# Tying a decoder block's background steps behind the newest weight piece

## The chip, the cores and the metric

The kernel runs on one core of one Trainium2 chip. The metric is the device time of one execution in microseconds. A core has engines that run side by side, each in its own program order: PE (TensorE) multiplies matrices and transposes, DVE (VectorE) and ACT (ScalarE) work on elements, POOL (GpSimd) does a few small things, SP issues most of the DMAs. They wait for each other by semaphores, so an instruction that is not ready holds up everything behind it on its engine.

## The reference

One decoder block for 256 tokens of width 2048, all in float32:

```python
mod = silu(c) @ w_ada + b_ada                  # 6 vectors of 2048
h = rmsnorm(x, g0) * (1 + sc_m) + sh_m
q, k, v, g_ret, u, gate_r, gate_s = split(h @ w_in)   # 1024 1024 2048 2048 1024 2048 2048
ret = head_group_norm(retention(rope(q), rope(k) * 128**-0.5, v))     # 8 heads
y_ret = (silu(g_ret) * ret) @ w_ret_out
y_ssm = gelu(s5_ssm(u, ...))                   # 64 groups of 16 channels, 64 complex states each
a, b = split(y_ssm @ w_s5_glu)
y = (sigmoid(gate_r) * y_ret + sigmoid(gate_s) * a * sigmoid(b)) @ w_out
x = x + gt_m * rmsnorm(y, g1)
h = rmsnorm(x, g2) * (1 + sc_f) + sh_f
a, b = split(h @ w_ffn_in)                     # 5632 each
x = x + gt_f * rmsnorm((silu(a) * b) @ w_ffn_out, g3)
```

## The kernel before

**Weight pieces.** Nearly all of the time goes into dense products with weights that are read once. A weight matrix is cut into pieces of 256 rows by 512 columns (512 KB). For one piece, `split_piece` issues the DMA into `raw` from SP, ACT copies it into a rounded part `hi` (L290), DVE subtracts to get the rest `lo` (the helper at L80), and `products` issues 12 matmuls: for each of the 2 blocks of 128 rows and 2 blocks of 128 tokens one on `hi` (L302), one of the activations' rest on `hi` (L303) and one on `lo` (L306). There are 3 buffers each of `hi` and `lo`, 5 of `raw`, 4 PSUM banks for products (`mm`) and 4 for everything else (transposes and small products).

**Stages.** The inner dimension of w_in is taken in three groups (`KG`), since the normalized input `h` becomes ready in three parts. In each group the columns in `EARLY` are multiplied; partial sums lie in the `spill` tiles, and the third group adds the last part to them in `early_evac`. There u is transposed (`uT`) and laid out for the S5 branch (`u_blocks`, 32 copies into `uS` on POOL, L852), q and k go through the rotary step (`rope_t`: on DVE two products into `rb`, one product and one sum on `spill`, for each of two token blocks, then four transposes into `ps_qk` on PE and a copy by ACT), and g_ret is gated and transposed (`ps_r`). The third group runs in the trace from about 235 to 400 us; then comes what is called the S5 stage here (gate r, w_ret_out and gate s, to about 720 us), then w_s5_glu and w_out, the second norm, and the FFN.

**Background.** Work that is not a weight piece is written as generators in two lanes. `mix` holds the S5 set-up (`s5_prep`), `u_blocks`, the retention heads (`heads`: scores `ps_s`, mask `sT`, outputs `ps_o`, statistics `bst` and `bag`) and the S5 groups (`s5_group`, eight of them, with small products `ps_bt`, `ps_v`, `ps_k`, `ps_y`). `ada` holds the modulation vectors: rows of w_ada come by DMA into `araw`, and DVE adds them up into `acc` (L202). After each piece `piece_done` ticks both lanes: each has a rate, and for each whole credit one step is issued. Deferred evacuations of finished columns (`later`) are issued three pieces after their column's end.

**The order.** A scheduler places each engine's instructions; the order in which the code issues them is its priority, and an instruction can move ahead of ones issued before it when it is thought to be ready earlier. `tc.issue_after(ins)` ties what is issued inside it behind `ins`. Before the change nothing in `piece_done` is tied.

Of the kernel before, what the change touches and what calls it, by code (L numbers as in the profile page):

```python
# [14 lines left out]
AF = mybir.ActivationFunctionType  # L15
# [37 lines left out]
def hybrid_block(ctx: ExitStack, tc: tile.TileContext, A, out, dbg=None):  # L53
# [25 lines left out]
    def tt(o, a, b, op):  # L79
        V.tensor_tensor(o, a, b, op=op)  # L80

    def slot(shape, dt, name):
        return slots.tile(shape, dt, tag="slot", name=name)
# [36 lines left out]
            while gen in self.gens:  # L120
                self.step()

    mix, ada = Lane(), Lane()

    def tick():
        mix.tick()
        ada.tick()

    late = []

# [154 lines left out]
    def split_piece(w, k0, KP, c0, keep=None, kept=None, tag="hi", hi=None):  # L285
        raw = wp.tile([P, KP, CW], F32, tag="raw", name="raw", bufs=RB)
        nc.sync.dma_start(raw, w[k0 * P:(k0 + KP) * P, c0:c0 + CW].rearrange("(k p) n -> p k n", p=P))
        if hi is None:
            hi = wp.tile([P, KP, CW], F32R, tag=tag, name="hi")
        S.activation(hi, raw, AF.Copy)  # L290
        lo = kept
        if lo is None:
            lo = keep if keep is not None else wp.tile([P, KP, CW], F32R, tag="lo", name="lo")
            tt(lo, raw, hi.bitcast(F32), ALU.subtract)
        return hi, lo

    def products(pst, lhs, hi, lo, k0, KP, ka, kb, toks):
        for k in range(KP):
            kt = k0 + k
            for t in toks:  # L300
                xh, xl = lhs(kt, t)
                T.matmul(pst[t], xh, hi[:, k, :], start=kt == ka, stop=False)  # L302
                T.matmul(pst[t], xl, hi[:, k, :], start=False, stop=False)  # L303
            for t in toks:
                xh, xl = lhs(kt, t)
                T.matmul(pst[t], xh, lo[:, k, :], start=False, stop=kt == kb - 1)  # L306

    later = []

# [2 lines left out]
            later.pop(0)[1]()  # L312

    def piece_done():
        tick()
        for it in later:
            it[0] -= 1
        while later and later[0][0] <= 0:
            later.pop(0)[1]()

    def defer(fn, *args):
        later.append([DEFER, lambda: fn(*args)])

    def mm_tile():
        return pmm.tile([P, CW], F32, tag="mm", name="mm")
# [330 lines left out]
    def s5_group(e):  # L656
# [12 lines left out]
        for g in range(2):  # L669
            pp = slice(64 * g, 64 * g + 64)  # L670
            S.activation(B4[pp, :, :, :, g, :].rearrange("p r t d h -> p (r t) d h"),
                         bp[pp].rearrange("p d r t h -> p (r t) d h"), AF.Copy)
            S.activation(B0[pp, :, :, g, :], bs[pp, e], AF.Copy)
            S.activation(CB[pp, :, :, 1:4, g, :].rearrange("p r t d h -> p (r t) d h"),
                         cp[pp].rearrange("p d r t h -> p (r t) d h"), AF.Copy)
            S.activation(CB[pp, :, :, 0, g, :], Cc[pp, e], AF.Copy)

        def mat(x, ri, t):
            return x[:, ri, t].rearrange("p d g h -> p (d g h)")
# [88 lines left out]
            yield  # L768

    def s5_all():  # L770
        yS.append(slot([P, 4, 4, 4, 32], F32, "yS"))
        for e in range(8):
            if e % 4 == 0:
                yield from s5_table(e // 4)
            yield from s5_group(e)
        dump("y", yS[0])
        yield from s5_out()
# [10 lines left out]
    def rope_t(src, dst):  # L788
        rope = ret[1]
        for t in range(2):  # L790
            sv = src[:, t, :].rearrange("p (h w d) -> p h w d", h=4, w=2)
            rb = ev("rb").rearrange("p (h w d) -> p h w d", h=4, w=2)
            for w in range(2):
                tt(rb[:, :, w, :], sv[:, :, 1 - w, :],
                   rope[:, t, 1:2, w * 64:w * 64 + 64].to_broadcast([P, 4, 64]), ALU.mult)
            s3 = src[:, t, :].rearrange("p (h d) -> p h d", h=4)
            tt(s3, s3, rope[:, t, 0:1, :].to_broadcast([P, 4, P]), ALU.mult)
            tt(src[:, t, :], src[:, t, :], rb.rearrange("p h w d -> p (h w d)"), ALU.add)
            ps = trp("ps_qk")
            for i in range(4):  # L800
                T.transpose(ps[:, i * P:(i + 1) * P], src[:, t, i * P:(i + 1) * P], ident)
            S.activation(dst[:, :, t * P:(t + 1) * P], ps.rearrange("p (i q) -> p i q", i=4), AF.Copy)

    def heads(hf, qk, vs):
        for i in range(4):
# [38 lines left out]
    def u_blocks(uT):  # L844
        uS.append(slot([P, NS, 64], F32, "uS"))
        uv = uS[0].rearrange("p (q ih v i) s -> p ih i v q s", q=4, ih=2, v=2)
        for i in range(4):
            for r in range(4):
                for v in range(2):
                    src = uT[32 * i:32 * i + 32, v].rearrange("p q (s r) -> p r q s", r=4)[:, r]  # L850
                    dst = uv[32 * (3 - r):32 * (3 - r) + 32, i // 2, i % 2, v]
                    G.tensor_copy(dst, src)  # L852
                yield

    def early_evac(gi, ci, pst):
# [12 lines left out]
        if ci == 1:  # L868
            uT = slot([P, 2, 4, NT], F32, "uT")
            for n in range(2):  # L870
                for t in range(2):
                    ps = trp("ps_u")
                    for i in range(4):
                        T.transpose(ps[:, i * P:(i + 1) * P], spill[0][:, n, t, i * P:(i + 1) * P], ident)
                    S.activation(uT[:, n, :, t * P:(t + 1) * P], ps.rearrange("p (i q) -> p i q", i=4), AF.Copy)
            mix.add(u_blocks(uT))
        if ci in (2, 3, 6, 7):
            if ci in (2, 6):
                keep["qk"] = slot([P, 2, 4, NT], F32, "qk")
            rope_t(sp, keep["qk"][:, ci % 2])  # L880
        if ci in (5, 9):
            hf = ci // 8
            vs[hf] = [spill[ci // 2][:, k] for k in range(2)]
# [36 lines left out]
    for gi, (k0, k1) in enumerate(KG):  # L920
        if gi + 1 < len(KG):
            nxt = ada_group(*KG[gi + 1])
            ada.add(nxt)
            ada.rate = 34 / (AR[gi] * NG[gi] * ((k1 - k0 + 1) // 2))
            if gi == 0:
                mix.add(prep)
                mix.rate = 0.14
        else:
            first_ctx.close()
            ret_tiles()  # L930
            af = ada.add(ada_f())
            ada.rate = 0.35
            mix.rate = 0.75
        for ci, off in enumerate(EARLY):
            if ci >= NG[gi]:
                continue
            g0 = gi
            while g0 and ci >= NG[g0 - 1]:
                g0 -= 1
            pst = linear(w_in, off, KG[g0][0], k1, h)  # L940
            defer(early_evac, gi, ci, pst)
        if gi + 1 < len(KG):
            ada.finish(nxt)
            flush()
            make_h(*KG[gi + 1])
            if gi == len(KG) - 2:
                mix.finish(prep)
# [4 lines left out]
    s5 = s5_all()  # L952
    s5_tiles()
    mix.add(s5)
    ada.rate = 0.5
    mix.rate = 0.75
    Mt = [slot([P, D], F32, "M") for _ in range(2)]

    def gate_evac(dst, n, pst):
# [232 lines left out]
```

## Time and profile before

| what | value |
|---|---|
| time, median of 3 runs | 1646.94 us (1644.99 to 1647.46) |
| profiled execution | 1647.59 us |
| its span in the trace | 1645.8 us |
| PE busy | 1592.4 us, 97% |
| PEld (weight loads of PE) | 1300.4 us, 79% |
| DVE busy | 1182.9 us, 72% |
| ACT busy | 780.8 us, 47% |
| POOL busy | 63.4 us, 4% |

The span is the time from the first to the last instruction that the profiler saw; 1.8 us of the profiled execution lie outside it. PE is busy nearly always, so what can be gained without taking work off PE is the 53.4 us of its span in which it is not busy, and what its clock loses.

### The profile page before, as it was taken

Reading aid. Unit: us, or ns where it says so; the run is one execution under the profiler, and the core shown is the slowest. Engines: PE = TensorE matmul, PEld = TensorE weight load, DVE = VectorE, ACT = ScalarE, POOL = GpSimd, SP = SyncE. Lnnn points to the kernel's source line nnn. Section 1 sums busy time; section 2 is a strip of 40 time slices with the busy share of each in tenths; the row PEclk is TensorE's granted clock in tenths of the full one; section 3 lists DMA queues with packets and bytes.
Section 4 is the critical chain, followed back from the end, with each engine's and each line's share of the span. In section 5 each row is a group of like instructions: output and inputs, shape, how many; then the busy total and the mean of one; then the engine's idle time right before and its main releaser. Section 6 shows DMA issues by size and latency. Waiting matters only on the chain.

```text
span 1645.8 us, 20564 instructions
## 1 busy us (share of the span) xinstructions
PE 1592.4 (97%) x7475; PEld 1300.4 (79%) x7475; DVE 1182.9 (72%) x1585; ACT 780.8 (47%) x1070; POOL 63.4 (4%) x84
## 2 busy tenths in 40 slices
PE   5999998999999999999998999999999999999997
PEld 2788886888778778788886788888888888888886
DVE  7889989888878988789966676477554455444454
ACT  4464443454656466544446544444444444344342
POOL 0200008010000000000000000000000000000000
PEclk9999999999999999999999999999999999999999
DMA  9999875765776867899985788688666666666663
GB/s 352 349 366 337 312 234 179 257 193 175 250 228 206 263 198 238 270 319 328 331 298 183 241 273 306 191 278 271 191 206 193 190 191 191 188 193 192 194 194 128
DMA packets 184005, 398.12 MB, mean 242 GB/s; under 512 B 12760, under 2 KB 14144, under 8 KB 183392
## 3 DMA queue, kind: packets, MB, share of 16 engines
q1 hardware_dynamic: 183360, 395.67, 73.7%
q0 software_dynamic: 544, 1.15, 0.3%
q8 instruction: 58, 0.95, 0.2%
q14 instruction: 43, 0.35, 0.1%
HBM read 394.67 MB, written 2.10 MB: 241 GB/s over the span
## 4 chain that ended last, share of the span: by engine, by line
PE 78%; DVE 8%; DMA 7%; issue 3%; ACT 2%; POOL 0%; SPq 0%; DVEq 0%; POOLq 0%; ACTq 0%
PE mm L306 25%; PE mm L302 25%; PE mm L303 25%; DMA araw<-in_w_ada_dram 4%; DVE lo L80 3%; DMA fraw<-in_w_ada_dram 1%; ACT hi L290 1%; DMA raw<-in_w_in_dram 1%; DVE acc L202 1%; DVE spill L80 1%; PE ps_a L1124 1%; PE ps_v L692 1%; DVE q L80 1%; DMA xs<-in_x_dram 0%; ACT Tz L701 0%
## 5 line engine op out<-in xcount | busy, mean ns | idle before, releaser
L290 ACT ACTIVATE hi<-raw 128x1024 fp32r<-128x1024 f32 x539 | 569.5, 1061 | 687.0 <-PE mm L303 611.9
L80 DVE TENSOR_TENSOR lo<-raw,hi 128x1024 fp32r<-128x1024 f32 x519 | 634.4, 1227 | 339.6 <-ACT hi L290 339.0
L302 PE MATMUL mm<-hi,h 128*128 128x512 f32 x1408 | 556.1, 395 | 1.9 <-ACT hi L290 1.3
L303 PE MATMUL mm<-hi,h 128*128 128x512 f32 x1408 | 550.4, 391 | 2.0 <-DVE h L80 2.0
L306 PE MATMUL mm<-lo,h 128*128 128x512 f32 x1376 | 426.9, 391 | 3.3 <-DVE lo L80 3.2
L302 PEld LDWEIGHTS mm<-hi,h 128*128 128x128 f32 x1408 | 265.2, 188 | 58.0 <-ACT hi L290 2.1
L303 PEld LDWEIGHTS mm<-hi,h 128*128 128x128 f32 x1408 | 265.4, 189 | 55.8 <-DVE h L80 2.4
L306 PEld LDWEIGHTS mm<-lo,h 128*128 128x128 f32 x1376 | 258.3, 188 | 61.7 <-DVE lo L80 7.4
L202 DVE SCALAR_TENSOR_TENSOR acc<-araw,cT,acc 128x1024 f32<-128x1024 f32 (+1 forms) x150 | 177.0, 1180 | 36.4 <-DMA araw<-in_w_ada_dram 36.2
L303 PE MATMUL mm<-hi,aT 128*128 128x512 f32 x348 | 135.5, 389 | 0.0
L302 PE MATMUL mm<-hi,aT 128*128 128x512 f32 x348 | 135.4, 389 | 0.0
L306 PE MATMUL mm<-lo,aT 128*128 128x512 f32 x348 | 108.1, 389 | 0.0
L302 PEld LDWEIGHTS mm<-hi,aT 128*128 128x128 f32 x348 | 65.3, 188 | 13.6
L303 PEld LDWEIGHTS mm<-hi,aT 128*128 128x128 f32 x348 | 65.3, 188 | 13.5
L306 PEld LDWEIGHTS mm<-lo,aT 128*128 128x128 f32 x348 | 65.3, 188 | 13.4
L202 DVE SCALAR_TENSOR_TENSOR acc<-gring,cT,acc 128x1024 f32<-128x1024 f32 x30 | 38.5, 1282 | 18.0 <-DMA gring<-in_w_ada_dram 17.9
L302 PE MATMUL mm<-hi,rT 128*128 128x512 f32 x128 | 51.1, 399 | 0.1
L303 PE MATMUL mm<-hi,rT 128*128 128x512 f32 x128 | 50.2, 392 | 0.0
L302 PE MATMUL mm<-hi,yg 128*128 128x512 f32 x128 | 50.2, 392 | 0.0
L302 PE MATMUL mm<-hi,mT 128*128 128x512 f32 x128 | 50.0, 391 | 0.0
L303 PE MATMUL mm<-hi,mT 128*128 128x512 f32 x128 | 50.0, 391 | 0.0
L303 PE MATMUL mm<-hi,yg 128*128 128x512 f32 x128 | 49.8, 389 | 0.0
(267 smaller groups left out, 1304.6 us busy)
## 6 DMA issues: line engine op xcount, KB each, us to landing
raw<-in_w_ffn_in_dram SPq DMA_DIRECT2D x178, 512.0 KB, 3.9
raw<-in_w_in_dram SPq DMA_DIRECT2D x176, 512.0 KB, 4.9
araw<-in_w_ada_dram SPq DMA_DIRECT2D x96, 512.0 KB, 4.8
raw<-in_w_ffn_out_dram SPq DMA_DIRECT2D x88, 512.0 KB, 4.6
araw<-in_w_ada_dram SPq DMA_DIRECT2D x64, 384.0 KB, 6.5
raw<-in_w_out_dram SPq DMA_DIRECT2D x34, 512.0 KB, 6.1
raw<-in_w_ret_out_dram SPq DMA_DIRECT2D x32, 512.0 KB, 5.1
raw<-in_w_s_glu_dram SPq DMA_DIRECT2D x32, 512.0 KB, 6.0
```

Source lines behind the costliest of these rows:

```text
L80: V.tensor_tensor(o, a, b, op=op)
L202: V.scalar_tensor_tensor(acc, raw, cT[:, kt:kt + 1], acc, op0=ALU.mult, op1=ALU.add)
L290: S.activation(hi, raw, AF.Copy)
L302: T.matmul(pst[t], xh, hi[:, k, :], start=kt == ka, stop=False)
L303: T.matmul(pst[t], xl, hi[:, k, :], start=False, stop=False)
L306: T.matmul(pst[t], xh, lo[:, k, :], start=False, stop=kt == kb - 1)
L692: T.matmul(pv[:, o:o + 64], BT[:, ri, t, :], uS[0][:, 4 * e + t, :], start=True, stop=True)
L1124: T.transpose(ps[:, j * P:(j + 1) * P], act[t][:, j * P:(j + 1) * P], ident)
```

## The change

After each `hi`, each `lo` and each piece's products the newest instruction of ACT, DVE and PE is noted (`mark`), and all that `piece_done` issues is tied behind these three (`behind`). The rotary step becomes a generator in the `mix` lane, with a pause between its DVE part and its transposes. `u_blocks` goes into a third lane, `low`, that is ticked only when `mix` is empty; its 32 copies go from POOL to ACT. `s5_group` has one pause more, between the ACT copies into `B` and the transposes into `ps_bt`. Evacuations of short columns are deferred by 2 pieces rather than 3. Rates: in the third group `ada` from 0.35 to 0.2 and `mix` from 0.75 to 1.0; in the S5 stage `ada` from 0.5 to 0.55 and `mix` from 0.75 to 0.9.

```diff
-    mix, ada = Lane(), Lane()
+    mix, low, ada = Lane(), Lane(), Lane()
     def tick():
-        mix.tick()
+        if mix.gens:
+            mix.tick()
+        else:
+            low.tick()
         ada.tick()
+    def mark(engine):
+        newest[engine] = last_ins(engine)
+    def behind():
+        es = ExitStack()
+        for ins in newest.values():
+            es.enter_context(tc.issue_after(ins))
+        return es
...
         S.activation(hi, raw, AF.Copy)
+        mark(mybir.EngineType.Activation)
...
             tt(lo, raw, hi.bitcast(F32), ALU.subtract)
+            mark(mybir.EngineType.DVE)
...
                 T.matmul(pst[t], xh, lo[:, k, :], start=False, stop=kt == kb - 1)
+        mark(mybir.EngineType.PE)
...
     def piece_done():
-        tick()
-        for it in later:
-            it[0] -= 1
-        while later and later[0][0] <= 0:
-            later.pop(0)[1]()
+        with behind():
+            tick()
+            for it in later:
+                it[0] -= 1
+            while later and later[0][0] <= 0:
+                later.pop(0)[1]()
...
             S.activation(CB[pp, :, :, 0, g, :], Cc[pp, e], AF.Copy)
+        yield
...
     def s5_all():
+        while low.step():
+            yield
...
             tt(src[:, t, :], src[:, t, :], rb.rearrange("p h w d -> p (h w d)"), ALU.add)
+            yield
             ps = trp("ps_qk")
...
-                    G.tensor_copy(dst, src)
+                    S.activation(dst, src, AF.Copy)
...
-            mix.add(u_blocks(uT))
+            low.add(u_blocks(uT))
...
-            rope_t(sp, keep["qk"][:, ci % 2])
+            mix.add(rope_t(sp, keep["qk"][:, ci % 2]))
...
-            ada.rate = 0.35
-            mix.rate = 0.75
+            ada.rate = 0.2
+            mix.rate = 1.0
...
-            defer(early_evac, gi, ci, pst)
+            defer(early_evac, gi, ci, pst, n=2 if k1 - KG[g0][0] <= 6 else DEFER)
...
-    ada.rate = 0.5
-    mix.rate = 0.75
+    ada.rate = 0.55
+    mix.rate = 0.9
```

How this moves instructions is shown at three places; line numbers in the rows of now are those of the changed kernel, where everything stands 16 to 25 lines lower (L302, L303, L306 are L318, L319, L322; L202 is L216). Pieces are counted from 0 over the whole kernel; the third group is pieces 64 to 111, the S5 stage 112 to 207.

**First rotary block, DVE** (the subtractions of pieces 75 to 77 and the rotary step of the first q column between them). Before:

```order
L80 TENSOR_TENSOR lo<-raw,hi 128x1024
L80 TENSOR_TENSOR rb<-spill,rope 128x4x64 x3
L80 TENSOR_TENSOR spill<-spill,rope 128x512
L80 TENSOR_TENSOR rb<-spill,rope 128x4x64
L80 TENSOR_TENSOR spill<-spill,rb 128x512
L80 TENSOR_TENSOR spill<-spill,rope 128x512
L80 TENSOR_TENSOR lo<-raw,hi 128x1024
L80 TENSOR_TENSOR spill<-spill,rb 128x512
L202 SCALAR_TENSOR_TENSOR acc<-araw,cT,acc 128x1024
```

Now:

```order
L80 TENSOR_TENSOR lo<-raw,hi 128x1024
L80 TENSOR_TENSOR rb<-spill,rope 128x4x64 x2
L80 TENSOR_TENSOR spill<-spill,rope 128x512
L80 TENSOR_TENSOR lo<-raw,hi 128x1024
L80 TENSOR_TENSOR spill<-spill,rb 128x512
L80 TENSOR_TENSOR rb<-spill,rope 128x4x64 x2
L80 TENSOR_TENSOR lo<-raw,hi 128x1024
L80 TENSOR_TENSOR spill<-spill,rope 128x512
L80 TENSOR_TENSOR spill<-spill,rb 128x512
L80 TENSOR_TENSOR spill<-spill,mm 128x512 x2
L80 TENSOR_TENSOR lo<-raw,hi 128x1024
```

The two token blocks of the step stood between two neighbouring `lo` but for one sum; now each stands in two parts, with a `lo` between them, and no more than three of its instructions stand between two `lo`.

**The same place, PE** (the matmuls of pieces 75 to 78). Before:

```order
L306 MATMUL mm<-lo,h 128x512 x2
L801 MATMUL ps_qk<-ident,spill 128x128 x8
L302 MATMUL mm<-hi,h 128x512
L303 MATMUL mm<-hi,h 128x512
L302 MATMUL mm<-hi,h 128x512
L303 MATMUL mm<-hi,h 128x512
L306 MATMUL mm<-lo,h 128x512 x2
L302 MATMUL mm<-hi,h 128x512
```

Now:

```order
L319 MATMUL mm<-hi,h 128x512
L322 MATMUL mm<-lo,h 128x512 x2
L823 MATMUL ps_qk<-ident,spill 128x128 x4
L318 MATMUL mm<-hi,h 128x512
L319 MATMUL mm<-hi,h 128x512
L318 MATMUL mm<-hi,h 128x512
L319 MATMUL mm<-hi,h 128x512
L322 MATMUL mm<-lo,h 128x512 x2
```

Eight transposes stood behind the `lo` matmuls of piece 75; now four stand behind piece 76, and the other four behind piece 77.

**Second rotary block, DVE** (between the `lo` of pieces 92 and 93, where the heads and the q column of the second half now come together). Before, around the rotary step of that column, between pieces 87 and 89:

```order
L80 TENSOR_TENSOR lo<-raw,hi 128x1024
L80 TENSOR_TENSOR rb<-spill,rope 128x4x64 x3
L80 TENSOR_TENSOR spill<-spill,rope 128x512
L80 TENSOR_TENSOR rb<-spill,rope 128x4x64
L80 TENSOR_TENSOR spill<-spill,rb 128x512
L80 TENSOR_TENSOR spill<-spill,rope 128x512
L80 TENSOR_TENSOR lo<-raw,hi 128x1024
L80 TENSOR_TENSOR spill<-spill,rb 128x512
```

Now:

```order
L80 TENSOR_TENSOR rb<-spill,rope 128x4x64
L847 BN_AGGR bag<-bst 128x2
L80 TENSOR_TENSOR rb<-spill,rope 128x4x64
L156 TENSOR_SCALAR rst<-bag 128x2
L80 TENSOR_TENSOR spill<-spill,rope 128x512
L851 SCALAR_TENSOR_TENSOR gnb<-bag,grs 128x2
L80 TENSOR_TENSOR spill<-spill,mm 128x512
L80 TENSOR_TENSOR sT<-ps_s,dec 128x256
L80 TENSOR_TENSOR sT<-ps_s,dec 128x128
L80 TENSOR_TENSOR spill<-spill,rb 128x512
L80 TENSOR_TENSOR spill<-spill,mm 128x512
L80 TENSOR_TENSOR lo<-raw,hi 128x1024
```

The statistics of a head (`bst` before these rows, `bag`, `rst`, `gnb`), a mask (`sT`) and an evacuation (`spill<-spill,mm`) now stand in one run with half of the rotary step.

**First S5 group, PE** (`ps_bt` are its eight transposes, `ps_v` the eight small products on their copies by ACT; the matmuls around them belong to pieces 121 and 122 before, 128 and 129 now). Before:

```order
L306 MATMUL mm<-lo,h 128x512
L685 MATMUL ps_bt<-ident,B_3489 128x128 x8
L306 MATMUL mm<-lo,h 128x512
L302 MATMUL mm<-hi,h 128x512
L692 MATMUL ps_v<-uS,BT 128x64 x4
L303 MATMUL mm<-hi,h 128x512
L692 MATMUL ps_v<-uS,BT 128x64 x4
L302 MATMUL mm<-hi,h 128x512
L303 MATMUL mm<-hi,h 128x512
L306 MATMUL mm<-lo,h 128x512 x2
```

Now:

```order
L704 MATMUL ps_bt<-ident,B_3456 128x128 x8
L319 MATMUL mm<-hi,h 128x512
L322 MATMUL mm<-lo,h 128x512 x2
L318 MATMUL mm<-hi,h 128x512
L319 MATMUL mm<-hi,h 128x512
L318 MATMUL mm<-hi,h 128x512
L319 MATMUL mm<-hi,h 128x512
L322 MATMUL mm<-lo,h 128x512 x2
L711 MATMUL ps_v<-uS,BT 128x64 x8
L318 MATMUL mm<-hi,h 128x512
```

Two matmuls stood between `ps_bt` and the first `ps_v`, and one more before the other four; now there are nine before all eight. At a later group (piece 171) the order is still close:

```order
L322 MATMUL mm<-lo,rT 128x512
L704 MATMUL ps_bt<-ident,B_3456 128x128 x8
L322 MATMUL mm<-lo,rT 128x512
L711 MATMUL ps_v<-uS,BT 128x64 x8
L318 MATMUL mm<-hi,rT 128x512
L319 MATMUL mm<-hi,rT 128x512
```

There the eight `ps_v` stand one `lo` matmul behind `ps_bt`.

## Rows read from the trace of the kernel before

**Rows 1.** The profile page: its span and the busy time of each engine.
```profile
span 1645.8 us, 20564 instructions
...
PE 1592.4 (97%) x7475; PEld 1300.4 (79%) x7475; DVE 1182.9 (72%) x1585; ACT 780.8 (47%) x1070; POOL 63.4 (4%) x84
```

**Rows 2.** The table by stretches: stretch, length, busy time per engine, granted TensorE clock, DMA share, GB/s.
```profile
240.00:280.00 40.00, 33.66 (x152) 27.55 (x152) 38.24 (x38) 14.96 (x18) 30.31 (x29) 0.91 0.60 187
...
340.00:400.00 60.00, 58.23 (x281) 48.26 (x280) 51.79 (x136) 31.67 (x47) 8.65 (x13) 1.00 0.54 158
400.00:720.00 320.00, 310.67 (x1696) 252.13 (x1696) 271.37 (x423) 185.52 (x348) 0.74 (x7) 1.00 0.75 244
720.00:860.00 140.00, 140.00 (x639) 116.24 (x638) 124.47 (x129) 66.07 (x80) 0.00 (x0) 1.00 0.91 318
```

**Rows 3.** Waits of PE from 240 to 720 us: total us, times, longest.
```profile
PE ps_qk L801 <- DVE spill L80: 6.3, 3, 3.0
PE mm L306 <- DVE lo L80: 3.4, 5, 1.3
PE ps_bt L685 <- ACT B L671: 1.7, 1, 1.7
PE ps_v L692 <- ACT BT L686: 1.2, 2, 0.9
PE ps_bt L685 <- issue: 1.2, 1, 1.2
PE mm L302 <- ACT hi L290: 1.1, 1, 1.1
...
PE ps_y L738 <- ACT Tz L701: 0.6, 1, 0.6
```

**Rows 4.** Chain of waits from 268 to 282 us: start, length, what.
```profile
274.25 0.43 PE mm L302
...
279.05 0.24 PE mm L302
...
281.79 0.23 PE mm L302
```

**Rows 5.** DVE, groups by shape, from 248 to 283 us.
```profile
L80 DVE TENSOR_TENSOR lo<-raw,hi 128x1024 fp32r<-128x1024 f32 x8 | 12.4, 1546 | 0.0
L80 DVE TENSOR_TENSOR rb<-spill,rope 128x256 f32<-128x256 f32 x8 | 6.5, 857 | 0.0
...
L80 DVE TENSOR_TENSOR spill<-spill,rope 128x512 f32<-128x512 f32 x4 | 4.5, 1122 | 0.0
```

**Rows 6.** DVE, groups by shape, from 286 to 320 us.
```profile
L80 DVE TENSOR_TENSOR lo<-raw,hi 128x1024 fp32r<-128x1024 f32 x13 | 15.7, 1218 | 0.0
...
L80 DVE TENSOR_TENSOR rb<-spill,rope 128x256 f32<-128x256 f32 x8 | 3.0, 418 | 0.0
...
L80 DVE TENSOR_TENSOR spill<-spill,rope 128x512 f32<-128x512 f32 x4 | 2.7, 684 | 0.0
```

**Rows 7.** POOL, groups by shape, the whole span.
```profile
L852 POOL COPY uS<-uT 32x256 f32<-32x256 f32 x32 | 33.2, 1055 | 104.3 <-ACT uT L875 103.4
```

**Rows 8.** ACT, groups by shape, the whole span.
```profile
L290 ACT ACTIVATE hi<-raw 128x1024 fp32r<-128x1024 f32 x539 | 569.5, 1061 | 687.0 <-PE mm L303 611.9 <-DMA raw<-in_w_in_dram 14.7 <-DMA raw<-in_w_ffn_in_dram 10.8
...
L744 ACT ACTIVATE yS<-ps_y 128x256 f32<-128x256 f32 x8 | 3.1, 385 | 5.8 <-PE ps_y L741 5.8
```

**Rows 9.** DVE, groups by shape, from 340 to 400 us.
```profile
L823 DVE BATCH_NORM_STATS2 bst<-ps_o 128x6 f32<-128x256 f32 x14 | 5.3, 420 | 0.4 <-PE ps_o L819 0.4
...
L828 DVE SCALAR_TENSOR_TENSOR gnb<-bag,grs 128x2 f32<-128x2 f32 x7 | 1.1, 161 | 4.1 <-POOL grs L143 4.1
```

**Rows 10.** DVE, groups by shape, from 400 to 720 us.
```profile
L80 DVE TENSOR_TENSOR lo<-raw,hi 128x1024 fp32r<-128x1024 f32 x97 | 117.7, 1219 | 14.2 <-ACT hi L290 14.1
L202 DVE SCALAR_TENSOR_TENSOR acc<-araw,cT,acc 128x1024 f32<-128x1024 f32 x45 | 57.6, 1281 | 26.3 <-DMA araw<-in_w_ada_dram 26.3
```

**Rows 11.** Timeline of PE from 33 to 44 us: start, length, engine, instructions.
```profile
35.97 0.41 PE L539 MATMUL ps_par<-ident,pd 32*128 32x32 f32 x4
```

More of the change, by code (lines that the diff above doesn't have):

```diff
@@ L121, in finish @@
                 self.step()
-    mix, ada = Lane(), Lane()
+    mix, low, ada = Lane(), Lane(), Lane()
     def tick():
-        mix.tick()
+        if mix.gens:
+            mix.tick()
+        else:
+            low.tick()
         ada.tick()
+    newest = {}
+    def mark(engine):
[5 more added lines that the diff above has]
+        return es
     late = []
@@ L314, in piece_done, with defer @@
     def piece_done():
-        tick()
-        for it in later:
-            it[0] -= 1
-        while later and later[0][0] <= 0:
-            later.pop(0)[1]()
-    def defer(fn, *args):
-        later.append([DEFER, lambda: fn(*args)])
+        with behind():
[4 more added lines that the diff above has]
+                later.pop(0)[1]()
+    def defer(fn, *args, n=DEFER):
+        later.append([n, lambda: fn(*args)])
     def mm_tile():
@@ L802, in rope_t @@
             S.activation(dst[:, :, t * P:(t + 1) * P], ps.rearrange("p (i q) -> p i q", i=4), AF.Copy)
+        yield
     def heads(hf, qk, vs):
```

## The prediction

> **What bounds the kernel now.** I read the page first: PE is busy for 1592.4 of 1645.8 us, every other engine far less [rows 1]. So the time is PE's own work plus what PE stands idle plus what it loses while its clock is low. The change takes no matmul away, so only the idle 53.4 us and the clock can pay for it. The table by stretches shows where the idle lies: from 720 to 860 us PE is busy for all of 140.00 us, but it misses 6.3 us between 240 and 280 (40.00 - 33.66), 1.8 between 340 and 400, and 9.3 in the S5 stage (320.00 - 310.67) [rows 2]. The rest lies at the start, in the second norm and at the end, which the change leaves alone. PE's waits from 240 to 720 us say who ends the gaps: the transposes of the rotary step waiting for DVE, 6.3 us in three gaps; a `lo` not ready, 3.4 in five; a `hi` not ready, 1.1; and the S5 groups' own products waiting for ACT or for their turn, 1.7 + 1.2 + 1.2 + 0.6 = 4.7 [rows 3].
>
> One more loss is not idle time. Between 240 and 280 us the granted clock averages 0.91 [rows 2], and the chain of waits shows why: after the last of these gaps a matmul takes 0.43 us where it later takes 0.24. That is the level of 1.2 GHz instead of 2.4, behind a stretch of gaps. The twelve matmuls of a piece take 279.05 - 274.25 = 4.80 us there and 281.79 - 279.05 = 2.74 right after [rows 4]: 2.1 us lost. The first rotary block therefore costs 6.3 + 2.1 = 8.4 us.
>
> **Why it stalls there.** A piece's `lo` is made when one of three `hi` buffers is free, since ACT's `hi` waits for PE nearly always (611.9 of 687.0 us of its idle time) [rows 8]. The buffer is freed two pieces before the new one is wanted, its own `lo` matmuls another 0.45 us, and the first `lo` matmul comes four `hi` matmuls (0.9 us) into the piece: 2 x 2.74 + 0.45 + 0.9 = 6.8 us. Of it 1.06 go to `hi` [rows 8] and 1.22 to `lo` [rows 6]. DVE may thus be held up by some 4.5 us between two `lo` without PE noticing. Before the change the rotary step stands in one run, four `rb` and three of the four-block operations, between two `lo`. At quiet durations that is 4 x 0.418 + 3 x 0.684 = 3.7 us [rows 6], inside the slack. But POOL copies `uS` at the same time, 32 x 1.055 us [rows 7], and while it does, `rb` takes 0.857, the product on `spill` 1.12 and `lo` itself 1.55 [rows 5]: 4 x 0.857 + 3 x 1.12 = 6.8 us, 2.3 over the slack. The transposes stand right behind a piece's last matmul, with no piece to wait behind.
>
> **The change part by part.**
>
> *First rotary block.* The copies leave POOL, so DVE runs at the quiet durations. The step is cut, so that two `rb` and one product, 2 x 0.418 + 0.684 = 1.5 us, stand between two `lo`, and each group of transposes stands a piece (2.74 us) later than its data is issued. Either half would do. I let 8.0 of the 8.4 us return, the clock's 2.1 among them, since without the gaps PE does not fall to the low level. The ends are 0 and 8.4.
>
> *The copies on ACT.* No row has this copy on ACT; the nearest are 128x256 from PSUM at 0.385 us and `hi` at 1.06 for 1024 columns [rows 8]. I take 0.385, so 32 x 0.385 = 12.3 us of ACT, bounds 8 and 34 (1.06 each). ACT is 15 us busy of 40 from 240 to 280 [rows 2], and the copies stand two by two behind a newest `hi`, in all 2 x 0.4 = 0.8 us at a time against the same slack. I cost them at nothing; the cover is ACT's idle time. Six of them stand in one run, 2.3 us, still below 4.5. At 1.06 each that run would be 6.4 us and cost 2 us once.
>
> *Second rotary block and heads, 340 to 400 us.* Of 1.8 us idle I let 0.8 return. The ties spread the heads' steps over more pieces, but they also make a new run on DVE between the `lo` of pieces 92 and 93: `bst` 2 x 0.420 [rows 9], `rb` 2 x 0.418 and four operations of 128x512 at 0.684 [rows 6] are 4.4 us, and four short operations on statistics, two masks and a wait of `gnb` for POOL (4.1 / 7 = 0.6 us) [rows 9] come on top, so that the run passes the slack by 1 to 2 us. The ends are 1.8 gained and 6.3 lost (this run stalls as the first block did).
>
> *S5 stage.* Of 9.3 us idle, 4.7 are of the S5 products, 4.5 of `hi` and `lo` [rows 3]. The first group has now nine matmuls where two stood between `ps_bt` and `ps_v`, some 2 us against ACT's copies, so that gap closes; at the later group that the order shows, the old neighbourhood stays. I let half of the 4.7 return. The `hi` and `lo` gaps come mostly where an `acc` stands in front of a `lo` and waits for its own DMA (26.3 us over 45 of them [rows 10]). A tie puts `acc` behind the newest `lo`, but not its DMA earlier; I let a third of 4.5 return. Together 2.4 + 1.5 = 3.9, rounded 4; ends 0 and 9.3.
>
> *What is added.* Seven small transposes (`ps_par`), which ran while PE was idle before the first piece, now stand among the pieces 7 and 9: four take 0.41 us [rows 11], so seven 0.7 (ends 0 and 2, if their chain on DVE holds up a `lo`). The rates move modulation work: 48 x (0.35 - 0.2) = 7.2 steps fewer in the third group, 96 x 0.05 = 4.8 more in the S5 stage, so 2.4 more in the next stage, where PE is never idle and DVE has 140 - 124.5 = 15.5 us left [rows 2] for 2.4 x 1.28 = 3.1. I take 0.5 (ends 0 and 2).
>
> **The sum.** 1647.6 (profiled execution: span 1645.8 and 1.8 outside) - 8.0 - 0.8 - 4.0 + 0.7 + 0.5 = 1636.0 us. That execution lies 0.65 us above the median of the runs, 1646.94; I do not correct for it.
>
> **The trace against a rule.** PE's weight loads are busy for 252.13 us in the S5 stage; at the 116.24 / 140 = 0.830 of the full stretch they would have 265.7, so they lack 13.6 us, which at 0.830 is 16.4 us of time where the matmul row shows 9.3 [rows 2]. The Trainium skill, page Perfetto Trace Analysis, section Identifying the Most-Contended Engine, says that matmul busy time is not a good measure since matmuls are pipelined, and to go by the weight loads' busy share. By it the same share of what is lost, 0.43 x 16.4 = 7.1 instead of 4, would return, and the sum would be 1633. I stay with 9.3, since the S5 products are many short matmuls whose own loads fill less.
>
> **Rivals.**
> - *Only the POOL copies matter.* The first block returns its 8.0, the ties elsewhere trade one gap for another: 1647.6 - 8.0 + 1.2 = 1640.8. For it: the 2.3 us over the slack are all POOL's; against: the order does change at the S5 groups. 0.25.
> - *Everything returns.* Idle and clock loss from 240 to 720 us go, and what is added hides: 1647.6 - 8.4 - 1.8 - 9.3 = 1628.1. For it: from 720 to 860 us PE is busy throughout beside a DVE that has more to do than in the S5 stage (0.89 of the time against 0.85) [rows 2]; against: the order at the later S5 group. 0.09.
> - *The ties don't do what they say.* The gap moves from the first block to the run at piece 92: 1647.6 - 8.0 + 6.3 + 1.2 = 1647.1. Against: only half of a rotary step is in that run and no POOL copy beside it. 0.09.
> - *Slower: DVE stands in order for DMAs in the S5 stage.* `acc` goes from 0.5 to 0.55 a piece there, and nothing tied behind the newest `lo` can be passed. DVE has 271.4 + 5 x 1.28 = 277.8 us of work in 320; it becomes the bound once it waits over 42 us for these DMAs (26.3 now, 0.58 each [rows 10]), and the kernel as a whole loses from 277.8 + 50 = 328 us, about 1.0 us per `acc`, since 8.8 - 1.2 = 7.6 are gained elsewhere. If the wait doubles to 1.16, 50 x 1.16 = 58: the stage takes 335.8, 15.8 more, and the kernel 1647.6 - 7.6 + 15.8 = 1655.8. Against: DMA engines are 0.75 busy there, and the third group asks for less. 0.09.
>
> **How the numbers follow.** The forecast has 0.48, its own range 1630 to 1639 (S5 stage from 1 to 9, first block from 7, the added from 0 to 3). 0.2% of 1646.94 is 3.3 us, about what can be told from no change: below 1643.6 is faster, above 1650.2 slower. Forecast, first and second rival are faster: 0.82; third within: 0.09; fourth slower: 0.09. The range reaches from 1627, so that it holds the second rival, to 1645, which leaves out the third and fourth: some 0.2 outside.
>
> **What would show it.** In the profile after: POOL has no `uS`; `rb` near 0.42 and `lo` near 1.22 us throughout the third group; no wait at `ps_qk` over 1 us and a granted clock of 1.00 from 240 to 280; a gap of 1 to 2 us near piece 92, twenty pieces (55 us) before the end of the third group; PE missing some 5 us in the S5 stage, with `ps_v` and `ps_bt` still among its waits. If `ps_qk` still waits, the first term is wrong; if the S5 stage misses 9 us or more, the third; if DVE waits over 42 us for `araw` there, the fourth rival is right. A sum below 1630 means that the ties freed pieces I took to be bound.

## The result and the profile after

The changed kernel takes 1637.16 us (median of 4 runs, 1635.04 to 1639.43), the kernel before 1646.14 (4 runs, 1644.99 to 1647.46): a ratio of 0.9945, with a 95% interval of 0.9928 to 0.9963. The forecast was 1636.0. The sum came out, but not by the terms that it was made of, and in part by luck. The profiled execution took 1636.99 us, with a span of 1635.0, 10.8 us less than before.

The table by stretches of the changed kernel (columns as in [rows 2]):

```profile
240.00:280.00 40.00, 40.00 (x194) 33.32 (x194) 32.64 (x42) 23.62 (x31) 0.00 (x0) 1.00 0.69 217
...
340.00:400.00 60.00, 60.00 (x281) 49.92 (x280) 46.16 (x93) 42.53 (x59) 5.43 (x10) 1.00 0.68 217
400.00:720.00 320.00, 312.77 (x1695) 255.28 (x1694) 280.36 (x450) 186.82 (x355) 0.85 (x8) 0.98 0.76 247
720.00:860.00 140.00, 139.43 (x634) 115.11 (x633) 124.34 (x127) 66.98 (x79) 0.00 (x0) 1.00 0.91 319
```

PE has no idle time left from 240 to 400 us, where it missed 6.3 and 1.8 us, and the clock is 1.00 there. From 400 to 720 it still misses 7.2 us (9.3 before), and its mean clock is now 0.98: there is a new stretch at the low level. PE's waits from 240 to 720 us, all of them, against [rows 3]:

```profile
PE ps_bt L704 <- ACT B L689: 2.3, 1, 2.3
PE mm L322 <- DVE lo L80: 1.5, 1, 1.5
PE ps_bt L704 <- issue: 1.2, 1, 1.2
PE ps_yt L782 <- DVE yS L80: 0.8, 2, 0.6
PE ps_y L757 <- ACT Tz L720: 0.6, 1, 0.6
PE ps_y L760 <- DVE Xs L80: 0.6, 1, 0.6
```

The rotary transposes wait no more. A fixed window hides where time was gained, since everything behind a gain starts earlier. Each piece has twelve dense matmuls in the trace, so the first of them dates the piece; the time from one such start to another compares the same pieces. (By these starts the third group lies from 222.4 to 387.8 us in the kernel before, 12 us earlier than its place was given above, so the windows do not cut the trace at the stages.)

| pieces | stage | before, us | after, us | difference |
|---|---|---|---|---|
| start to 0 | up to the first dense matmul | 37.0 | 37.1 | +0.1 |
| 0 to 64 | first two groups | 185.4 | 185.5 | +0.1 |
| 64 to 112 | third group | 165.5 | 154.8 | -10.6 |
| 112 to 208 | S5 stage | 323.3 | 323.5 | +0.2 |
| 208 to 256 | w_s5_glu, most of w_out | 137.0 | 138.1 | +1.2 |
| 256 to the end | rest of w_out, second norm, FFN | 797.7 | 796.0 | -1.8 |

(The last row's two parts: 690.9 to 689.2 up to piece 500, and 106.8 in both behind it. The sum, -10.8, is the difference of the spans.) All of the gain that can be put down to the change lies in the third group; the S5 stage, which was to give 4, gave nothing. The -1.8 at the end can't be: kernel 1 below, which is the same as the kernel before from piece 256 on, took 689.4 from there to piece 500, so two executions of the same code differ by 1.5 us there.

### The profile page after: what moved, and what is told of

Read it like the earlier page. It is cut to its first block, busy times and chain, and to the rows that moved or that the text cites. A ratio compares the mean times of both kernels' runs of the same rounds, so it can differ in the third digit from the quotient of the medians.

```text
span 1635.0 us, 20550 instructions
## 1 busy us (share of the span) xinstructions
PE 1593.6 (97%) x7475; PEld 1304.0 (80%) x7475; DVE 1173.8 (72%) x1585; ACT 800.7 (49%) x1102; POOL 28.7 (2%) x52
## 4 chain that ended last, share of the span: by engine, by line
PE 88%; DVE 5%; DMA 3%; ACT 2%; issue 2%; POOL 0%; SPq 0%; DVEq 0%; POOLq 0%; ACTq 0%
PE mm L318 27%; PE mm L319 27%; PE mm L322 27%; DVE lo L80 1%; PE ps_v L711 1%; ACT hi L304 1%; DMA fraw<-in_w_ada_dram 1%; DMA raw<-in_w_out_dram 1%; PE ps_a L1147 1%; DMA raw<-in_w_in_dram 1%; DVE acc L216 1%; PE ps_bt L704 1%; PE ps_y L760 0%; DMA araw<-in_w_ada_dram 0%; ACT Tz L720 0%
## 5 line engine op out<-in xcount | busy, mean ns | idle before, releaser
L318 PE MATMUL mm<-hi,h 128*128 128x512 f32 x1408 | 556.4, 395 | 1.2 <-ACT h L437 1.2
L319 PE MATMUL mm<-hi,h 128*128 128x512 f32 x1408 | 550.4, 391 | 2.0 <-DVE h L80 2.0
L322 PE MATMUL mm<-lo,h 128*128 128x512 f32 x1376 | 425.1, 390 | 0.1
L319 PEld LDWEIGHTS mm<-hi,h 128*128 128x128 f32 x1408 | 265.2, 189 | 56.0 <-DVE h L80 2.8
L318 PEld LDWEIGHTS mm<-hi,h 128*128 128x128 f32 x1408 | 264.9, 188 | 56.3 <-issue 1.4
L322 PEld LDWEIGHTS mm<-lo,h 128*128 128x128 f32 x1376 | 258.3, 188 | 55.8 <-DVE lo L80 1.0
L216 DVE SCALAR_TENSOR_TENSOR acc<-araw,cT,acc 128x1024 f32<-128x1024 f32 (+1 forms) x150 | 175.5, 1170 | 0.2
L319 PE MATMUL mm<-hi,aT 128*128 128x512 f32 x348 | 135.5, 389 | 0.0
L318 PE MATMUL mm<-hi,aT 128*128 128x512 f32 x348 | 135.4, 389 | 0.0
L322 PE MATMUL mm<-lo,aT 128*128 128x512 f32 x348 | 108.1, 389 | 0.0
L318 PEld LDWEIGHTS mm<-hi,aT 128*128 128x128 f32 x348 | 65.3, 188 | 13.7
L319 PEld LDWEIGHTS mm<-hi,aT 128*128 128x128 f32 x348 | 65.3, 188 | 13.5
L322 PEld LDWEIGHTS mm<-lo,aT 128*128 128x128 f32 x348 | 65.2, 188 | 13.5
L318 PE MATMUL mm<-hi,rT 128*128 128x512 f32 x128 | 51.9, 405 | 0.0
L319 PE MATMUL mm<-hi,rT 128*128 128x512 f32 x128 | 50.9, 398 | 0.0
L318 PE MATMUL mm<-hi,yg 128*128 128x512 f32 x128 | 50.2, 392 | 0.0
L319 PE MATMUL mm<-hi,mT 128*128 128x512 f32 x128 | 50.0, 391 | 0.0
L318 PE MATMUL mm<-hi,mT 128*128 128x512 f32 x128 | 49.9, 390 | 0.0
L319 PE MATMUL mm<-hi,yg 128*128 128x512 f32 x128 | 49.8, 389 | 0.0
L322 PE MATMUL mm<-lo,rT 128*128 128x512 f32 x128 | 40.7, 398 | 1.5 <-DVE lo L80 1.5
```

The costliest lines, as they stand in the source:

```text
L216: V.scalar_tensor_tensor(acc, raw, cT[:, kt:kt + 1], acc, op0=ALU.mult, op1=ALU.add)
```

## The experiments

All edits are to the changed kernel unless the kernel before is named. Times are medians, ratios (with 95% intervals) are to the kernel before, measured beside each, where its median was 1645.76 us (1, 2, 3, 8), 1645.66 (4, 5, 6, 9) and 1643.64 (7, 10, 11, 12). Stage times are by pieces, from the one profiled execution of each, and differences of them are taken before rounding. Those of 1, 4 and 5 took 3.0, 4.9 and 2.8 us more than their kernels' medians. Where kernels have the same code in a stage, the third group agrees within 0.1 us (154.8 in the changed kernel, 8 and 10), the S5 stage within 0.4 (323.3 before, 323.7 in 1), the first 64 pieces only within 2.3.

**1. The copies on ACT alone** (kernel before).

```diff
-                    G.tensor_copy(dst, src)
+                    S.activation(dst, src, AF.Copy)
```

> The kernel before with one edit: the 32 uS copies run on ACT instead of POOL; nothing is tied, the rotary step is not cut, rates as before. Theory A (slack: the first rotary block stalled because POOL stretched a run of DVE work past the slack of the next lo, and either quiet durations or a cut step mends it): rb near 0.42 and lo near 1.22 us from 240 to 280, PE missing at most 2.5 us there (6.3 before), clock 1.00, total 6 to 8 us shorter than before, 1638 to 1641. Theory B (the order: eight transposes right behind a piece, in front of the next, wait for the whole rotary step however fast it is): PE still misses 4 us or more there and less than 4 us return, 1642.5 or more.

Measured: 1642.91 us, ratio 0.9987 (0.9976 to 0.9998); third group 163.6. The waits of PE and two groups of DVE from 240 to 283 us:

```profile
PE ps_qk L801 <- DVE spill L80: 3.1, 2, 2.6
PE mm L302 <- ACT hi L290: 0.8, 1, 0.8
```

```profile
L80 DVE TENSOR_TENSOR lo<-raw,hi 128x1024 fp32r<-128x1024 f32 x10 | 12.1, 1222 | 9.4 <-ACT hi L290 9.4
L80 DVE TENSOR_TENSOR rb<-spill,rope 128x256 f32<-128x256 f32 x8 | 3.0, 416 | 0.0
```

DVE runs at the quiet durations as expected (0.416 and 1.222, against 0.857 and 1.546 in [rows 5]), yet half of the wait stays, and now `lo` waits 9.4 us for `hi`. Theory A fell: `hi` is late, so `lo` is, and the rotary step stands behind them; the copies have to be out of the way on ACT too. Theory B came near by its numbers (PE misses 3.9 us from 240 to 280), but its reason, the transposes behind an uncut step, falls with (7), where they wait for nothing.

**2. The copies back on POOL.**

```diff
-                    S.activation(dst, src, AF.Copy)
+                    G.tensor_copy(dst, src)
```

> The changed kernel with one edit undone: the 32 uS copies are back on POOL (in the lane low, so that most come behind the rotary blocks). Theory A: the cut step alone covers the first block too; rb and lo beside a copy take 0.8 and 1.5 us, PE still misses under 1.5 us between 240 and 340, total within 2 us of the changed kernel, 1635 to 1639. Rival (only the move of the copies pays): the rotary gaps and the low clock come back, 5 us or more slower than the changed kernel, 1642 or more.

Measured: 1638.34 us, ratio 0.9958 (0.9942 to 0.9973); third group 160.7. From 240 to 282 us:

```profile
PE mm L322 <- DVE lo L80: 3.9, 3, 2.7
PE ps_qk L823 <- DVE spill L80: 0.7, 1, 0.7
```

The total is as theory A expected, but not by its reason: the third group loses 5.8 us, and DVE, slowed by POOL (`rb` 0.861 us), is late with `lo`. The lane `low` did not bring the copies behind the rotary blocks: all 32 stand at pieces 72 to 80. The total stays since the S5 stage is shorter, 318.5 us instead of 323.5; why is told with that stage below.

**3. No ties.**

```diff
-        for ins in newest.values():
-            es.enter_context(tc.issue_after(ins))
```

> The changed kernel without the ties: behind() ties to nothing, everything else stays (lanes, pauses, ACT copies, rates). Theory A: the gain of the third group comes from the cut step and the copies, not the ties: third group within 1.5 us of the changed kernel's; in the S5 stage, where the change gained nothing net, 0 to 3 us either way; total 1634 to 1640. Rival (the ties carry the gain): 5 us or more slower than the changed kernel, 1642 or more, with DVE waiting over 15 us for araw in the S5 stage again (0 with ties, 26.3 in the kernel before).

Measured: 1651.20 us, ratio 1.0036 (1.0022 to 1.0050), slower than the kernel before; third group 162.2, S5 stage 324.2. The rival was right. The timeline of ACT shows the reason (start, length, instructions of one line in a row):

```profile
253.12 3.66 ACT L873 ACTIVATE uS<-uT 32x256 f32<-32x256 f32 x6
256.80 1.06 ACT L302 ACTIVATE hi<-raw 128x1024 fp32r<-128x1024 f32 x1
257.88 3.71 ACT L873 ACTIVATE uS<-uT 32x256 f32<-32x256 f32 x6
261.62 1.06 ACT L302 ACTIVATE hi<-raw 128x1024 fp32r<-128x1024 f32 x1
```

Six copies between two `hi`, 3.7 us, make ACT's round 4.8 us where a piece needs 2.74. Five rounds of about this length use up all that ACT was ahead, and PE waits for `hi`:

```profile
PE mm L316 <- ACT hi L302: 2.9, 3, 1.5
```

**4. Ties to ACT's `hi` alone, and 5. ties to DVE's `lo` alone.** In each two of the three `mark` calls are left out.

> The changed kernel with the ties to ACT's newest hi alone (none to DVE's lo or PE's products). Theory E (the ties pay on ACT: without them the uS copies stand in runs of six, 2.3 us, behind each hi of pieces 74 to 79, ahead of the next hi, and the pieces wait): the third group (pieces 64 to 111) takes within 2 us of the changed kernel's 154.8 us (162.2 without ties); the rest as without ties; total 1640 to 1645. Rival F (they pay on DVE, where acc, waiting for its DMA, otherwise stands ahead of a lo): third group and total stay within 2 us of the kernel without ties, 1649 to 1653.

> The changed kernel with the ties to DVE's newest lo alone. Theory E: the third group stays near 162 us, since ACT's order is that without ties; DVE's wait for araw in the S5 stage falls below 5 us (23.1 without ties) but that alone brings 0 to 4 us; total 1647 to 1651. Rival F: total 1640 to 1643.

Measured: 1645.97 us (0.9995, 0.9983 to 1.0007), third group 155.0, S5 stage 330.0 (in an execution of 1650.87 us, the longest of twelve); and 1642.38 us (0.9977, 0.9966 to 0.9987), third group 160.5, S5 stage 323.0. The stretch from 240 to 280 us, first with the ACT tie, then with the DVE tie:

```profile
240.00:280.00 40.00, 40.00 (x194) 33.35 (x193) 32.73 (x43) 24.11 (x32) 0.00 (x0) 1.00 0.71 223
```

```profile
240.00:280.00 40.00, 36.83 (x170) 28.48 (x169) 26.52 (x36) 35.02 (x51) 0.00 (x0) 1.00 0.56 169
```

The third group is the ACT tie's, as theory E has it. What the tie does is seen in the copies: without it all 32 stand at pieces 72 to 79, in (3) and in (5); with it a run of six and two pairs stand up to piece 81, and the other 22 at pieces 105 to 116. Against no ties (1651.20) the ACT tie alone is worth 5.2 us by the medians (its total lies 1 us above theory E's range), and the DVE tie alone 8.8, where the theory had 0 to 4 and was wrong. Where these 8.8 us arise is not shown: the profiled executions of (3) and (5) differ by 4.1 us only: (5) takes 1.7 less in the third group, 1.2 in the S5 stage and 2.3 from piece 256 to 500, and 1.5 more up to piece 64. Neither kernel has the tie to PE's products, which no run tries alone; 5.2 and 8.8 make up the 14.0 us between (3) and the changed kernel, each uncertain by 2 to 3 us. DVE's wait for its own DMAs in the S5 stage, with the ACT tie alone:

```profile
DVE acc L216 <- DMA araw<-in_w_ada_dram: 21.6, 17, 3.3
```

With the DVE tie that row is gone from the answer.

**6. The ties alone** (put into the kernel before).

> The kernel before with the ties alone: the rotary step uncut and at its old place, the copies on POOL, the old rates and deferral. Theory G (ties and the cut step need each other: a tied, uncut rotary step is a run of 6.4 us at quiet durations between two lo, more beside POOL's copies, with eight transposes right behind a piece): third group 162 to 169 us (165.5 before, 154.8 changed), DVE's wait for araw in the S5 stage under 5 us, S5 stage within 3 us of before; total 1642 to 1649. Rival (the ties are the change): third group 159 or less, total 1641 or less.

Measured: 1642.45 us, ratio 0.9978 (0.9965 to 0.9991); third group 165.4, S5 stage 317.4. As expected, but for the S5 stage, which gains 5.9 us by the ties alone, and where DVE waits for no modulation DMA. In the third group the old waits stand:

```profile
PE ps_qk L816 <- DVE spill L80: 7.4, 3, 3.0
```

**7. The rotary step uncut.**

```diff
-            mix.add(rope_t(sp, keep["qk"][:, ci % 2]))
+            for _ in rope_t(sp, keep["qk"][:, ci % 2]):
+                pass
```

> The changed kernel with the rotary step uncut: it runs at once in the evacuation as before, all else (ties, copies on ACT, lanes, rates) as changed. Theory G (under ties the copies and the cut each carry part of the third group's 10.6 us: 165.5 us with neither, 160.7 with the cut alone, 154.8 with both): 158 to 163 us for pieces 64 to 111, with PE waiting for ps_qk again; total 1640 to 1645, if the S5 stage, which starts with fewer steps behind, stays within 3 us. Rival (with DVE at quiet durations a run of 5 us does no harm): third group under 156.5 us, no wait for ps_qk over 1 us.

Measured: 1631.62 us, ratio 0.9922 (0.9907 to 0.9937); third group 154.6, no wait for `ps_qk`, S5 stage 316.5. Theory G fell: with the copies on ACT behind `hi`, the step that the prediction's arithmetic was about need not be cut. Now 24 of the 32 copies stand at pieces 72 to 81, beside the step, but behind a first run of six they stand two by two, so that ACT's round is 2.3 us:

```profile
261.75 1.22 ACT L875 ACTIVATE uS<-uT 32x256 f32<-32x256 f32 x2
262.99 1.06 ACT L304 ACTIVATE hi<-raw 128x1024 fp32r<-128x1024 f32 x1
```

The third group by what each kernel has (before, 1 and 6 with the old lanes, rates and deferral, the others with the new):

| copies on | ties | rotary step | pieces 64 to 112, us |
|---|---|---|---|
| POOL | none | uncut (before) | 165.5 |
| ACT | none | uncut (1) | 163.6 |
| POOL | all | uncut (6) | 165.4 |
| POOL | all | cut (2) | 160.7 |
| ACT | none | cut (3) | 162.2 |
| ACT | ACT's | cut (4) | 155.0 |
| ACT | DVE's | cut (5) | 160.5 |
| ACT | all | uncut (7) | 154.6 |
| ACT | all | cut (changed) | 154.8 |

No run changes the lanes, rates and deferral alone, so what they give to the third group is not shown apart; the 4.8 us between (6) and (2) are the cut's and theirs together.

**8. The S5 stage's rates as before.**

```diff
-    ada.rate = 0.55
-    mix.rate = 0.9
+    ada.rate = 0.5
+    mix.rate = 0.75
```

> The changed kernel with the rates of the S5 stage as before: ada 0.5 instead of 0.55, mix 0.75 instead of 0.9. Theory C (the S5 stage gained nothing since the faster rates pile acc, bp, q and the evacuations M between two lo at pieces 168 to 173, where one cluster of gaps and a low clock cost 8.8 us): that cluster shrinks to under 4 us, the clock stays at 1.00 from 400 to 720, the stage is 2 to 5 us shorter, total 1632 to 1635.5, unless the S5 work that is left over at the stage's end shows as a gap there. Rival D (the cluster comes from weight pieces whose DMA is late, since SP waits in order for the ring's buffers): stage within 1.5 us of the changed kernel's, and the cluster moves with the group.

Measured: 1641.98 us, ratio 0.9977 (0.9967 to 0.9988). The stage takes 313.5 us instead of 323.5, more of a gain than theory C had; up to its end, at 692 us, no wait of PE in it is over 1.3 us and the granted clock is 1.00. So the cluster is gone, and has not moved with the group as by rival D it should have. (Pieces 168 to 176 take 21.9 us instead of 37.7, but no S5 product falls among them here, so these two do not compare.) Yet 11 S5 steps are left over at the stage's end by the rates, 10 modulation rows stand behind piece 208 in the trace (4 in the changed kernel), and they come at once: pieces 208 to 256 take 148.0 instead of 138.1, and 256 to 500 take 694.4 instead of 689.2. Theory C's "unless" decided the total.

**9. Modulation steps moved to the third group.**

```diff
-            ada.rate = 0.2
+            ada.rate = 0.3
-    ada.rate = 0.55
+    ada.rate = 0.5
```

> The changed kernel with ada.rate 0.3 instead of 0.2 in the third group and 0.5 instead of 0.55 in the S5 stage: 4.8 steps of the modulation vectors move from the S5 stage to the third group, the number left for later stays, mix stays at 0.9 (the run with both old rates left 11 S5 steps and 4 more modulation steps over, which were then issued at once). Theory C (the cluster at pieces 168 to 175 comes from acc, bp, q and M piled between two lo): pieces 112 to 207 take 316 to 320 us (323.5 changed, 313.5 with both old rates), the third group up to 1.5 us more, total 1631 to 1635. Rival D (late weight DMAs of the shared ring, whatever the rate): pieces 112 to 207 take 322 to 325, total 1636 to 1639.

Measured: 1628.53 us (4 runs, 1627.88 to 1630.50), ratio 0.9893 (0.9875 to 0.9910), better than both kernels. The S5 stage takes 314.6 us, pieces 168 to 176 take 29.6, the third group still 154.8. Both the stage and the total are below theory C's ranges, since the stage gained more than it had; from piece 208 on the kernel takes as long as the changed one within 0.3 us. The S5 stage by stretch, and PE's waits from 560 to 600 us:

```profile
400.00:720.00 320.00, 316.68 (x1734) 258.96 (x1734) 285.83 (x457) 189.26 (x358) 0.84 (x8) 1.00 0.76 250
```

```profile
PE ps_bt L704 <- ACT B L689: 1.1, 1, 1.1
```

**10. One pair of products moved.** The rates stay as changed; w_ret_out's evacuations come one piece later.

```diff
-    defer(ret_evac, n, linear(w_ret, n * CW, 0, KD, rl))
+    defer(ret_evac, n, linear(w_ret, n * CW, 0, KD, rl), n=4)
```

> The changed kernel, rates as changed, with the evacuations of w_ret_out's columns (the two M products) deferred by 4 pieces instead of 3, so that the pair behind piece 170 no longer stands among acc, q and bp between two lo. Theory C (the pile of DVE work between two lo makes the cluster): pieces 168 to 175 take 29 to 32 us (37.7 changed, 29.6 with the moved rate), total 1629 to 1633. Rival H (five modulation rows more in the ring make weight pieces late there, whatever stands between two lo): 35 us or more, total 1636 to 1639.

Measured: 1633.33 us, ratio 0.9933 (0.9917 to 0.9950); pieces 168 to 176 take 31.5 us, in the range of theory C, the total a third of a us above it. The S5 stage takes 317.8 us. Rival H, late DMAs through more modulation rows, is out: the rows were as many (50 from piece 112 to 207 in both kernels).

**11. The same step once more, 12. S5 groups in halves.** The first has `ada.rate` 0.4 and 0.45, the second is kernel 9 with a pause behind each half of `bp` and `cp` and `mix.rate` 1.05.

> As the kernel with the moved rate, once more the same step: ada.rate 0.4 in the third group, 0.45 in the S5 stage, the sum unchanged. If fewer modulation rows help by their number: S5 stage 1 to 3 us shorter than 314.6, third group 0 to 2 longer, total 1626 to 1629. If only the place of the one cluster mattered: within 1.5 us of 1628.5, or slower by what a run of 6.8 us on DVE behind piece 101 costs (up to 3 us).

> The kernel with the moved rate, and the S5 groups' bp and cp issued in halves (a pause after each of the four triples q, q, bp or cp), mix.rate 1.05 instead of 0.9 for the 16 more steps. If runs on DVE between two lo still cost the S5 stage its last 3.3 us of idle time: pieces 112 to 207 take 312 to 314 us (314.6 with the moved rate), total 1626 to 1628. If what is left are the groups' own waits (B, BT, Xs): within 1 us of 1628.5.

Measured: 1632.85 us (0.9929, 0.9913 to 0.9945), S5 stage 316.8, third group 156.1; and 1633.69 us (0.9934, 0.9918 to 0.9950), S5 stage 319.0. Neither did what was expected: both are slower than kernel 9. From 240 to 720 us PE waits for no `lo` in the second, but longer for the groups' own chain, 2.1 us at three places where kernel 9 has 1.0:

```profile
PE ps_y L760 <- DVE Xs L80: 2.1, 3, 1.3
```

The rest of the 4.4 us by which its S5 stage is longer no run explains.

## Why the prediction was right, and where it was not

*First rotary block, 8.0 of 8.4 forecast: all 8.4 came back, but the reason given was half wrong.* "Either half would do" was the step that failed. The copies' move alone brings 1.8 us in the third group (1), the cut with the copies on POOL at most 4.8 (2), and the cut is worth nothing once they are moved and tied (7). What does it is the move together with the tie to ACT, as (3) and (4) show with the cut, and (1) and (7) without it; the new lanes and rates are in all of these but (1). The mechanism on DVE was seen rightly (`rb` and `lo` fall back to their quiet durations). But the prediction gave the gain to the move or the cut and counted the copies on ACT as covered by its idle time. ACT has that time; without the tie the copies take it ahead of `hi`.

*The copies on ACT, taken at 0.385 us and costing nothing.* They take 0.657:

```profile
L875 ACT ACTIVATE uS<-uT 32x256 f32<-32x256 f32 x32 | 19.7, 657 | 0.4
```

That is inside the bounds (8 to 34 us for 32 of them). The cost is nothing only by the ties; "two by two behind a newest `hi`" was the condition that the prediction named, and (3) shows what its loss costs.

*Second rotary block and heads, 0.8 forecast: 1.8 came.* The run at piece 92 was there, and did not stall. By the trace the `lo` of piece 92, ahead of the run, was ready 7.5 us before its first matmul, and that of piece 93, behind it, still 3.9: the slack was more than the 4.5 us worked out from bare pieces, which leaves out the heads' products that PE does between pieces.

*S5 stage, 4.0 forecast: 0 came, the term that failed.* The two causes named were real: PE's waits for `ps_v` are gone, and DVE's 26.3 us of waiting for modulation DMAs [rows 10] are gone altogether; the ties alone gain 5.9 us (6). The gain was then given back at one place. Pieces 168 to 176 hold as many of the S5 groups' small products in both kernels (64) and take 37.7 us instead of 28.3, while the rest of the stage takes some 9 us less. DVE behind piece 170 in the changed kernel:

```profile
559.68 1.22 DVE L80 TENSOR_TENSOR lo<-raw,hi 128x1024 fp32r<-128x1024 f32 x1
560.82 0.76 DVE L80 TENSOR_TENSOR q<-bs,lam 128x256 f32<-128x256 f32 x2
561.49 1.28 DVE L216 SCALAR_TENSOR_TENSOR acc<-araw,cT,acc 128x1024 f32<-128x1024 f32 x1
562.68 0.42 DVE L80 TENSOR_TENSOR bp<-q 128x256 f32<-128x256 f32 x1
563.02 0.68 DVE L80 TENSOR_TENSOR M<-M,mm 128x512 f32<-128x512 f32 x1
563.62 0.76 DVE L80 TENSOR_TENSOR q<-bs,lam 128x256 f32<-128x256 f32 x2
564.29 0.68 DVE L80 TENSOR_TENSOR M<-M,mm 128x512 f32<-128x512 f32 x1
564.89 0.42 DVE L80 TENSOR_TENSOR bp<-q 128x256 f32<-128x256 f32 x1
565.22 1.22 DVE L80 TENSOR_TENSOR lo<-raw,hi 128x1024 fp32r<-128x1024 f32 x1
```

4.4 us stand between two `lo`, at a place where the `lo` before was ready only 1.26 us ahead of its first matmul. PE waits 1.5 us for that `lo` and, behind the same work, 2.3 for `B`; its granted clock falls (0.87 on average from 560 to 600 us), as the chain of waits from 564 to 580 us shows:

```profile
569.32 1.97 PE ps_bt L704 x8
...
571.72 3.31 PE ps_v L711 x16
...
575.56 0.43 PE mm L319
...
578.91 0.23 PE mm L319
```

The eight transposes take 1.97 us, the small products 3.31, and dense matmuls 0.43 until 578.9, the level of 1.2 GHz. The prediction had this arithmetic, a slack against what stands between two `lo`, and used it in the third group, but not in the S5 stage, where it counted parts of the old gaps as closed and no new one as opened. Its own sign for this term, 9 us or more missing from 400 to 720, would have passed it: PE misses 7.2 there, and part of the loss is in the clock.

That the cause is the pile, not the ring of weight buffers, rests on (9) and (10), which move different parts of it and both mend it: the work on `bp` then has at most 2.5 us between two `lo`. Neither the length of such a run nor the rates decide alone. Earlier in the changed kernel DVE does other work for 7 us between two `lo`, and PE waits for nothing, since the `lo` before was ready 7.7 us ahead:

```profile
518.84 1.22 DVE L80 TENSOR_TENSOR lo<-raw,hi 128x1024 fp32r<-128x1024 f32 x1 [2.36 <-ACT hi L304]
...
527.72 1.22 DVE L80 TENSOR_TENSOR lo<-raw,hi 128x1024 fp32r<-128x1024 f32 x1
```

Kernel 2 has the same run of 4.4 us at the same place, but PE waits 0.6 us for `lo` and 2.0 for `B`, and pieces 168 to 176 take 33.6 us. And kernel 7 has the rates of the change, yet its S5 groups begin at piece 125 rather than 128, so that other steps fall together: the same eight pieces take 27.3 us, and its stage gains 6.8 (316.5). The pile is thus a chance of what the lanes bring to one place, which the faster rates of the change did not force.

*What is added, 1.2 forecast.* +0.2 up to piece 64 and +1.2 from 208 to 256: 1.4.

*The total, 1636.0 forecast.* That it was met within 1.2 us is in part luck: the third group gave 1.8 us more than the 8.8 of its two terms, and the two executions differ by 1.8 behind piece 256, hardly more than two of the same code do; together these make up for most of the 4 that the S5 stage did not give.

*The rivals.* That only the POOL copies matter is refuted by (1). That everything returns was wrong for the changed kernel, but 9 is at 1628.5 where it forecast 1628.1. That the ties only move the first block's gap to piece 92 is refuted by the missing stall there. The slower rival, DVE standing in order for its DMAs, went the other way: tied, DVE waits for no modulation DMA in that stage. It is without the tie to DVE that it waits, 21.6 us (4), and without any that the kernel is slower than before (3). By the estimate that the prediction worked out from the rule of the Trainium skill (Perfetto Trace Analysis, Identifying the Most-Contended Engine), 7 us of the S5 stage would have come back rather than 4. Neither did: PE's weight loads rose from 252.13 to 255.28 us in that window, and its matmuls from 310.67 to 312.77, while the same pieces took as long as before.

## What to carry to other kernels

Moving background work to an engine with idle time helps only if the order keeps it behind the work that feeds the bottleneck: here the move alone was worth 1.8 us in its stage (1), the ties alone nothing (6), and both, with the new lanes and rates, 10.8 (7). Where several lanes are ticked by rates, look at the worst place and not at the mean: at how much stands between two feeding instructions there, and how far ahead the first of them is. A run of 4.4 us behind a `lo` that was 1.26 us ahead went with a loss of 9 us; one of 7 us behind a `lo` 7.7 us ahead brought no wait. A lane's rate also has a lower end, since what is left over at a stage's end comes at once (8).

## What the runs showed of the hardware

The granted clock fell in the changed kernel behind two gaps of 1.5 and 2.3 us, which end at 566.5 and 569.3 us (0.87 on average from 560 to 600 us), and less in kernel 2, with gaps of 0.6 and 2.0 at the same group (0.96); it did not in kernel 10, with gaps of 0.6 and 1.6 (1.00). A strided copy of 32 partitions by 256 elements took 0.657 us on ACT and 1.055 on POOL (0.978 in kernel 2); with the copies on ACT, DVE's two-input operations on SBUF took 0.416 us (`rb`), beside those on POOL 0.86.
